# Holding the load of row tile 10 for the transpose of row tile 9 instead of row tile 7

## The chip, the cores and the metric

The kernel runs on one core of a Trainium2 chip. The time is the device time of one execution in microseconds (us), of which the median of several runs is given. The profile is of one execution, with its own time.

## What is computed

```python
batch, m, k, n = 16, 512, 1024, 768
y1 = np.matmul(x, w1)      # x: [16, 512, 1024], w1, w2: [1024, 768], all float32
y2 = np.matmul(x, w2)
out = np.tanh(y1) * y2     # [16, 512, 768], float32
```

Seen as one matrix, x has 8192 rows: 64 row tiles of 128 rows. Both products have the same x, so the weights stand side by side as 1536 columns, three blocks of 512: "a" (the first 512 of w1), "g" (the last 256 of w1 and of w2) and "b" (the first 512 of w2).

## The kernel before, in words

**Tiles.** The first four row tiles (0 to 3) are multiplied plainly, while the weights arrive. The other 60 are taken in 20 triples of three row tiles; the first triple holds rows 4, 5, 6, the second 7, 8, 9, the third 10, 11, 12. For a triple the matrices are seen as 3 row tiles by 2 halves of K, times 2 halves of K by 3 column blocks. That would be 18 block products; the kernel makes 15, out of sums of blocks. A product, called p0 to p14, is four matmuls of 128x512 (`product`, L455). Its left operand is either a half of a transposed row tile or a sum of such halves, called S and a number whose bits name the halves (`A_SUMS`, L13; `x_sum`, L420). S3 is made of the two halves of the triple's first row tile, S11 is S3 less the second half of its second row tile, S15 is made of S11. S11 is read by S15 and p5, S15 by p6 and S31. The right operand is a weight block or a sum B of weight blocks, made once (`w_sum`, L412).

**What a row tile goes through.** From row tile 7 on, each goes through these steps:
- L, the load: GpSimd issues a DMA from memory that also casts to fp16, into one of 8 buffers `xh` (`load_x`, L362).
- D, the sum of absolute values for a check of the inputs' range, on ScalarE (L390).
- T, the transpose: SyncE issues a DMA transpose from `xh` into one of 12 buffers `xT` (L387).
- S, the sums of halves, on VectorE (L421).
- The products on TensorE (L457), with results in PSUM, in 8 banks.
- Copies and sign changes of partial results on ScalarE (`copy`, `seed`, L461), additions of them on VectorE (`add`, L467), tanh on ScalarE (`t`, `th`, L470), the last multiplication on VectorE (`m`, `mh`, L475).
- The store, issued by SyncE (L427).

**Which order.** The order of the products on TensorE is written out by hand (`PE_ORDER`, L69, and `sequence` after it), and neighbouring triples overlap in it. For the other engines a planner (`Planner`, L75 to L224) runs when the kernel is built. It plays the kernel through with assumed costs, and each engine takes the operation that can start first; among those within 0.02 us the one that is due first, and one that is more urgent is waited for (`pick`, L126). It also gives each chain of partial results a PSUM bank. Each engine then executes its list strictly in the planner's order, waiting where an operand isn't there yet: one operation that waits holds up all that stands behind it on its engine.

**What the planner is told of the transposes.** For most transfers it reckons a landing itself. For the transposes of rows 7 to 15 the landing times are written out (`LANDING`, L254; used at L786). They are numbers for the planner's ordering alone: nothing on the chip waits for them.

**The rows' order and the hold.** The rows of the second triple are loaded in the order 7, 9, 8 (`TURNS`, L253; `rows`, L255), those of the third in the order 10, 11, 12. The loads of each triple from the third on are held back: ahead of the triple's first load GpSimd runs a small cast (`hold_loads`, L500, L501) that reads one column of a transposed row tile into a dummy. GpSimd's list is in order, so the loads behind the cast start only when that transpose has landed. Before the change the cast reads the first row tile of the triple before: row 7 for the loads of 10, 11 and 12; row 10 for those of 13, 14 and 15; and so on (L779 to L783):

```python
        if n >= FREE and n % 3 == 0:
            held_by = rows[BY_PE + n - 3]
            op(f"H{mt}", {"pool": 0.1}, None, [f"T{held_by}"], hold_loads, held_by, issued=[before])
            before = f"H{mt}"
```

The load of row 12 also waits until its buffer, that of row 6, is free, and so for the check D of row 6 on ScalarE.

**How operations are named here.** "add4 of the first triple" is operation add4 in the table `C_OPS` for that triple; so with p, S, mh and the others.

Of the kernel before, what the change touches and what calls it, by code (L numbers as in the profile page):

```python
# [74 lines left out]
class Planner:  # L75
# [9 lines left out]
    def op(self, name, engines, due, needs, fn, *args, behind=(), issued=(), chains=(), xfer=0.0, latency=None, seeds=False,  # L85
           lands=None, hold=0.0):
        assert name not in self.ops, name
        self.ops[name] = dict(engines=engines, due=due, needs=[n for n in needs if n], behind=[n for n in behind if n], issued=[n for n in issued if n], fn=fn, args=args,
                              chains=chains, xfer=xfer, latency=latency, seeds=seeds, lands=lands, hold=hold)
        for c in chains:  # L90
            self.chains.setdefault(c, {"left": 0, "bank": None, "end": 0.0, "act": 0.0, "dve": 0.0})["left"] += 1
# [135 lines left out]
def kernel(  # L227
# [18 lines left out]
    BY_PE = HEAD + 3  # L246
# [4 lines left out]
    FILL = 512, 512, 256  # L251
    FREE = 3
    TURNS = (2, 0, 1), (0, 2, 1)  # L253
    LANDING = {7: 35.9, 9: 37.2, 8: 38.4, 10: 45.0, 11: 46.3, 12: 47.7, 13: 54.0, 14: 55.4, 15: 56.8}  # L254
    rows = list(range(HEAD)) + [HEAD + 3 * i + r for i in range(TRIPLES) for r in (TURNS[i] if i < len(TURNS) else (0, 1, 2))]  # L255
    turn = {mt: n for n, mt in enumerate(rows)}
    S_AHEAD, HALVED = 4.0, 4
# [47 lines left out]
    def xh_before(mt):  # L305
        return next((m for m in rows[turn[mt] - 1:1:-1] if xh_place(m) == xh_place(mt)), None)
# [398 lines left out]
    for i in range(TRIPLES):  # L705
# [10 lines left out]
        for o in C_OPS:  # L716
# [22 lines left out]
            if kind in ("t", "th"):  # L739
                lo, n = (0, F) if kind == "t" else (F, G)  # L740
# [11 lines left out]
            else:  # L752
                lo, n, at = (0, F, 0) if kind == "m" else (F, G, G)
# [21 lines left out]
    for n, mt in enumerate(loads):  # L775
        back = xh_before(mt)
        free = [] if back is None else ([f"PT{back}0", f"PT{back}1"] if back < BY_PE else [f"T{back}"]) + ([f"D{back}"] if back >= HEAD else [])
        before = f"L{loads[n - 1]}" if n else last_early
        if n >= FREE and n % 3 == 0:  # L779
            held_by = rows[BY_PE + n - 3]  # L780
            op(f"H{mt}", {"pool": 0.1}, None, [f"T{held_by}"], hold_loads, held_by, issued=[before])
            before = f"H{mt}"
        op(f"L{mt}", {"pool": 0.58}, None, [], load_x, mt, issued=[before], behind=free, xfer=XX)  # L783
    for n, mt in list(enumerate(rows))[BY_PE:]:
        op(f"T{mt}", {"sp": 0.05}, None, [f"L{mt}"], transpose, mt, issued=[f"T{rows[n - 1]}"] if n > BY_PE else [],
           behind=xt_readers[mt - XT_BUFS] if mt >= XT_BUFS and mt - XT_BUFS != HEAD - 1 else [], xfer=1.2, latency=2.0, lands=LANDING.get(mt))  # L786
    for mt in range(HEAD, MT):
# [128 lines left out]
```

## Time and profile before

| | us |
|---|---|
| median of 3 runs | 297.25 |
| the 3 runs | 297.2, 297.25, 298.45 |
| the profiled execution's own time | 297.27 |
| its span, from the first to the last instruction | 295.7 |
| TensorE busy in the span | 289.4 |
| VectorE busy | 255.9 |
| ScalarE busy | 224.3 |
| GpSimd busy | 43.2 |

A line of a timeline gives the start in us from the span's start, the duration in us, the engine (PE is TensorE, PEld its weight load, DVE is VectorE, ACT is ScalarE, POOL is GpSimd, SPq the queue of SyncE), the line of the kernel, the operation, what it writes and reads (`out<-in`, buffer numbers left out), the shapes, and how many like it are merged in the line. In square brackets stand the engine's idle time just before it and what ended that. The durations of neighbours overlap a little, since an engine begins the next operation while the last one drains. A line of a DMA issue ends with the KB of one and the us from issue to landing. A line of the windows gives from:to, the length, then for each engine its busy us and the count of its instructions, the granted clock of TensorE, the DMA share and GB/s.

### The profile page before, as it was taken

Reading aid. Unit: us, or ns where it says so; the run is one execution under the profiler, and the core shown is the slowest. Engines: PE = TensorE matmul, PEld = TensorE weight load, DVE = VectorE, ACT = ScalarE, POOL = GpSimd, SP = SyncE. Lnnn points to the kernel's source line nnn. Section 1 sums busy time; section 2 is a strip of 40 time slices with the busy share of each in tenths; the row PEclk is TensorE's granted clock in tenths of the full one; section 3 lists DMA queues with packets and bytes.
Section 4 is the critical chain, followed back from the end, with each engine's and each line's share of the span. In section 5 each row is a group of like instructions: output and inputs, shape, how many; then the busy total and the mean of one; then the engine's idle time right before and its main releaser. Section 6 shows DMA issues by size and latency. Waiting matters only on the chain. (4 is left out here: it accounts for less than half of the span.)

```text
span 295.7 us, 4593 instructions
## 1 busy us (share of the span) xinstructions
PE 289.4 (98%) x1374; PEld 132.5 (45%) x1374; DVE 255.9 (87%) x552; ACT 224.3 (76%) x454; POOL 43.2 (15%) x94
## 2 busy tenths in 40 slices
PE   7999999999999999999999999999999999999993
PEld 3445444444444444444444444444444444444442
DVE  1679999999989898898989988898888989898884
ACT  2698599799878878877888788677777767778451
POOL 0065112202202022022021120220210100000000
PEclk9999999999999999999999999999999999999999
DMA  6999998999999999999999999999999999041234
GB/s 216 388 323 204 184 153 157 205 240 235 241 177 175 191 242 203 254 174 285 208 200 284 233 230 217 259 270 254 223 296 239 221 280 300 15 162 54 108 142 163
DMA packets 84858, 63.63 MB, mean 215 GB/s; under 512 B 62816, under 2 KB 67168, under 8 KB 84832
## 3 DMA queue, kind: packets, MB, share of 16 engines
q1 hardware_dynamic: 73888, 45.10, 58.8%
q0 software_dynamic: 9936, 16.65, 35.6%
q10 hardware_dynamic: 1008, 1.57, 1.5%
q8 instruction: 11, 0.18, 0.3%
q14 instruction: 15, 0.12, 0.2%
HBM read 39.85 MB, written 25.17 MB: 220 GB/s over the span
## 5 line engine op out<-in xcount | busy, mean ns | idle before, releaser
L457 PE MATMUL bank<-b,early_x 128*128 128x512 f16 x640 | 148.2, 379 | 0.0
L457 PEld LDWEIGHTS <-early_x 128*128 128x128 f16 x800 | 78.2, 98 | 94.5 <-DVE early_x L421 0.3
L467 DVE TENSOR_TENSOR bank<-bank,arena 128x512 f32<-128x512 f32 x100 | 69.7, 697 | 14.7 <-ACT arena L461 12.3
L461 ACT ACTIVATE arena<-bank 128x512 f32<-128x512 f32 x100 | 57.8, 596 | 16.4 <-PE bank L457 16.2
L475 DVE TENSOR_TENSOR o<-o,bank 128x256 f32<-128x256 f32 (+1 forms) x128 | 62.0, 517 | 6.5 <-ACT o L470 4.8
L390 ACT ACTIVATE junk<-xh 128x1024 f16<-128x1024 f16 x60 | 63.4, 1057 | 0.1
L457 PEld LDWEIGHTS <-xT 128*128 128x128 f16 x400 | 39.1, 98 | 46.8 <-issue 0.3
L457 PE MATMUL bank<-b,xT 128*128 128x512 f16 x240 | 58.3, 379 | 0.0
L470 ACT ACTIVATE o<-bank 128x256 f32<-128x256 f32 (+1 forms) x80 | 34.7, 439 | 27.1 <-DVE bank L467 23.7
L457 PE MATMUL bank<-wh,xT 128*128 128x512 f16 x160 | 41.1, 379 | 0.0
L457 PE MATMUL bank<-wh,early_x 128*128 128x512 f16 x160 | 40.9, 379 | 0.0
L362 POOL DMA_DIRECT2D xh<-in_x_dram x61 | 32.4, 542 | 14.9 <-ACT junk L390 7.3
L421 DVE TENSOR_TENSOR early_x<-early_x,xT 128x512 f16<-128x512 f16 x80 | 33.6, 422 | 0.5
L470 ACT ACTIVATE o<-arena 128x512 f32<-128x512 f32 x40 | 25.1, 629 | 8.5 <-DVE arena L467 8.5
L501 POOL CAST held<-xT 128x1 f32<-128x1 f16 x18 | 5.4, 301 | 162.0 <-DMA xT<-xh 162.0
L461 ACT ACTIVATE bank<-bank 128x512 f32<-128x512 f32 x40 | 21.5, 570 | 4.5 <-PE bank L457 3.6
L430 PE MATMUL bank<-wh,xT 128*128 128x512 f16 x72 | 19.6, 379 | 0.2
L421 DVE TENSOR_TENSOR early_x<-xT,xT 128x512 f16<-128x512 f16 x40 | 16.8, 421 | 0.0
L421 DVE TENSOR_TENSOR early_x<-xT,early_x 128x512 f16<-128x512 f16 x40 | 16.8, 420 | 0.0
L467 DVE TENSOR_TENSOR arena<-bank,arena 128x512 f32<-128x512 f32 x20 | 13.7, 687 | 3.0 <-ACT arena L461 3.0
L467 DVE TENSOR_TENSOR bank<-arena,bank 128x512 f32<-128x512 f32 x20 | 13.8, 692 | 0.3 <-PE bank L457 0.3
L467 DVE TENSOR_TENSOR arena<-arena,bank 128x512 f32<-128x512 f32 x20 | 13.6, 681 | 0.0
(51 smaller groups left out, 139.9 us busy)
## 6 DMA issues: line engine op xcount, KB each, us to landing
out_dram<-o SPq DMA_DIRECT2D x59, 384.0 KB, 5.6
xh<-in_x_dram POOLq DMA_DIRECT2D x58, 256.0 KB, 6.7
arena<-in_w_dram SPq DMA_DIRECT2D x12, 256.0 KB, 5.7
early_x<-in_x_dram SPq DMA_DIRECT2D x8, 256.0 KB, 4.8
arena<-in_w_dram ACTq DMA_DIRECT2D x4, 256.0 KB, 5.8
wh<-in_w_dram POOLq DMA_DIRECT2D x8, 128.0 KB, 5.4
xT<-xh SPq DMA_TRANSPOSE x57, 4.6
out_dram<-o SPq DMA_DIRECT2D x3, 256.0 KB, 2.5
```

Source lines behind the costliest of these rows:

```text
L362: pin(nc.gpsimd.dma_start(xh(mt)[:, cols], xf[mt][:, cols]))
L390: pin(nc.scalar.activation(junk[:, :src.shape[-1]], src, ACT.Abs, scale=scale, accum_out=sums[:, column:column + 1]))
L421: pin(engine[e].tensor_tensor(x_operand(i, v), x_operand(i, a), x_operand(i, b), OP[how]))
L430: pin(nc.tensor.matmul(bank(chain)[:, :rhs.shape[-1]], xt(mt)[:, k, :], rhs, start=first, stop=k == KO - 1, skip_group_check=True))
L457: pin(nc.tensor.matmul(place(i, dst), x_operand(i, a)[:, k, :], w_rhs(b, k), start=begins and k == 0, stop=k == KH - 1, skip_group_check=T ...
L461: pin(nc.scalar.activation(place(i, dst), place(i, src), ACT.Copy, scale=float(sign)))
L467: pin(nc.vector.tensor_tensor(place(i, dst), a, b, ALU.add if signs == (1, 1) else ALU.subtract))
L470: pin(nc.scalar.activation(out_tile(HEAD + 3 * i + r)[:, lo:lo + n], place(i, src)[:, :n], ACT.Tanh, scale=float(sign)))
L475: pin(nc.vector.tensor_tensor(o, o, place(i, src)[:, at:at + n], ALU.mult))
L501: pin(nc.gpsimd.tensor_copy(held, xt(mt)[:, 0, :1]))
```

## The change

The cast ahead of the third triple's loads reads row 9 instead of row 7. All later holds are as they were: `n == FREE` is true only for n = 3, which is row tile 10. And the planner is told other landing times for rows 8 and 10 to 15. By these, S11 of the second triple, which needs row 8, can no longer be planned at once behind add128 of the first triple; it stands behind add128 and mh2 of the first triple.

```diff
-    LANDING = {7: 35.9, 9: 37.2, 8: 38.4, 10: 45.0, 11: 46.3, 12: 47.7, 13: 54.0, 14: 55.4, 15: 56.8}
+    LANDING = {7: 35.9, 9: 37.2, 8: 39.4, 10: 47.4, 11: 48.3, 12: 49.2, 13: 55.0, 14: 56.3, 15: 57.6}
...
         if n >= FREE and n % 3 == 0:
-            held_by = rows[BY_PE + n - 3]
+            held_by = rows[BY_PE + n - 3 + (n == FREE)]
             op(f"H{mt}", {"pool": 0.1}, None, [f"T{held_by}"], hold_loads, held_by, issued=[before])
```

## The prediction

> **What bounds the kernel now.** I read the page's engine lines, then the windows of the trace, then who waits for whom, and then the timelines of VectorE, TensorE, GpSimd and the DMA queue around the change.
>
> ```profile
> span 295.7 us, 4593 instructions
> PE 289.4 (98%) x1374; PEld 132.5 (45%) x1374; DVE 255.9 (87%) x552; ACT 224.3 (76%) x454; POOL 43.2 (15%) x94
> ```
> ```profile
> 0.00:14.50 14.50, 12.72 (x69) 6.17 (x70) 5.77 (x15) 6.84 (x12) 0.69 (x6) 1.00 0.84 300
> 14.50:284.00 269.50, 269.50 (x1267) 122.62 (x1266) 243.44 (x525) 214.19 (x436) 42.48 (x88) 1.00 0.99 213
> 291.00:295.70 4.70, 0.16 (x2) 0.00 (x0) 1.06 (x4) 0.00 (x0) 0.00 (x0) 1.00 0.41 142
> ```
>
> The first number of a window row is its length, the second TensorE's busy time. From 14.5 to 284 us TensorE is busy for 269.50 us of 269.50, at a granted clock of 1.00. So TensorE's fixed list of matmuls is the bound, and a wait that the change removes from VectorE, GpSimd or a DMA buys nothing as long as TensorE didn't wait for it. What TensorE has idle is 14.50 - 12.72 = 1.8 us in the lead-in and the 4.7 us tail; the change starts at row tile 10, after 36 us, and touches neither. That is why I look for losses only: **from which point does a later row tile 10 make TensorE wait, and by how much?**
>
> The views of the stretch, first GpSimd's loads and the transposes that they feed:
>
> ```profile
> 35.86 0.37 POOL L501 CAST held<-xT 128x1 f32<-128x1 f16 x1 [7.13 <-DMA xT<-xh]
> 36.37 1.05 POOL L362 DMA_DIRECT2D xh<-in_x_dram  x2
> 38.38 0.53 POOL L362 DMA_DIRECT2D xh<-in_x_dram  x1 [0.96 <-ACT o L470]
> 46.47 0.20 POOL L501 CAST held<-xT 128x1 f32<-128x1 f16 x1 [7.56 <-DMA xT<-xh]
> 47.00 1.59 POOL L362 DMA_DIRECT2D xh<-in_x_dram  x3 [0.33 <-ACT bank L461]
> ```
> ```profile
> 33.78 1.24 SPq L387 DMA_TRANSPOSE xT<-xh  x1
> ```
> ```profile
> xT<-xh SPq DMA_TRANSPOSE x1, 3.3
> ```
> ```profile
> 35.12 1.27 SPq L387 DMA_TRANSPOSE xT<-xh  x1
> ```
> ```profile
> xT<-xh SPq DMA_TRANSPOSE x1, 3.2
> ```
> ```profile
> 40.93 1.23 SPq L387 DMA_TRANSPOSE xT<-xh  x1
> ```
> ```profile
> xT<-xh SPq DMA_TRANSPOSE x1, 5.4
> ```
> ```profile
> 50.71 1.23 SPq L387 DMA_TRANSPOSE xT<-xh  x1
> ```
> ```profile
> xT<-xh SPq DMA_TRANSPOSE x1, 4.2
> ```
>
> Start plus time to landing gives the transposes of rows 9, 8, 10 and 13, in this order: 33.78 + 3.3 = 37.08, 35.12 + 3.2 = 38.32, 40.93 + 5.4 = 46.33 and 50.71 + 4.2 = 54.91 us. The cast at 35.86 is the hold for row 7; the loads of rows 10 and 11 follow at 36.37, that of row 12 at 38.38. The cast at 46.47 is the next hold, for row 10.
>
> **Part 1, the hold.** Nothing is added; one GpSimd cast reads row 9 instead of row 7. Row 9 lands at 37.08. With row 7's spacing (cast 0.1 after the landing, load 0.51 after the cast's start, 36.37 - 35.86) the cast starts at 37.18 and the load of row 10 is issued at 37.69, 1.32 us later. Row 11 stands behind it on GpSimd's queue and moves as much; row 12, issued at 38.38, moves only to 38.74, when the other two (1.05 us) are through. On SP's queue the transposes of 10, 11 and 12 stand behind, then that of 13; the stores come after. When row 10 then lands is not in this trace, so it has two ends. From the same round: the whole 1.32 us goes through, 46.33 + 1.32 = 47.65. From the next round, whose three loads leave back to back as they now will here: 54.91 - 47.00 = 7.91 us after the load, 37.69 + 7.91 = 45.60, earlier than now. I take 47.4, near the upper end, because that row is the same round with the same neighbours, and the lower end only because row 12 moves by 0.36 us, not 1.32.
>
> Who waits for it? VectorE, which runs its list in order:
>
> ```profile
> 47.21 0.43 DVE L421 TENSOR_TENSOR early_x<-xT 128x512 f16<-128x512 f16 x1
> 47.55 0.70 DVE L467 TENSOR_TENSOR bank<-bank,arena 128x512 f32<-128x512 f32 x1
> 48.15 0.89 DVE L421 TENSOR_TENSOR early_x<-early_x,xT 128x512 f16<-128x512 f16 x2
> 48.95 0.75 DVE L475 TENSOR_TENSOR o<-o,bank 128x256 f32<-128x256 f32 x2
> 49.61 0.69 DVE L467 TENSOR_TENSOR bank<-arena,bank 128x512 f32<-128x512 f32 x1
> ```
> ```profile
> 50.78 1.03 PE L457 MATMUL bank<-wh,xT 128*128 128x512 f16 x4
> 53.37 1.03 PE L457 MATMUL bank<-b,early_x 128*128 128x512 f16 x4
> ```
>
> The sum S3 of the third triple (rows 10 to 12) reads row 10 first, at 47.21; S11 and S15 at 48.15 read rows 10 and 11. Their own reader on TensorE is p6 at 53.37, far off. But whatever is queued behind S3 moves with it: add128, S11, S15, two mh, and at 49.61 the addition add4 of the first triple, which ends at 49.61 + 0.69 = 50.30. In the planner's assignment of PSUM banks add4 is the last to read bank 0 before p7 of the third triple takes that bank at 50.78: **0.48 us of slack**, the smallest that I find behind S3. (p7 itself needs row 12 by 50.78; its transpose would land about 1.3 us later than now, by 49.4.) How much of the 0.48 is usable? The nearest that TensorE follows VectorE in this trace:
>
> ```profile
> 30.82 0.42 DVE L421 TENSOR_TENSOR early_x<-early_x,xT 128x512 f16<-128x512 f16 x1
> 31.33 2.75 PE L457 MATMUL bank<-b,early_x 128*128 128x512 f16 x12
> ```
>
> That is 31.33 - 31.24 = 0.09 us. So VectorE may slip by 0.48 - 0.10 = 0.38 us and row 10 may land until 47.21 + 0.38 = 47.59 with no cost. At my 47.4 VectorE slips 0.2 us: cost 0. At the upper end, 47.65: 0.06 us. Beyond that each us of lateness costs TensorE a us, for good, since TensorE has no idle time later to win it back. Below nothing it cannot go.
>
> **Part 2, S11 of the second triple behind add128 and mh2.** It and its neighbours:
>
> ```profile
> 38.24 0.69 DVE L467 TENSOR_TENSOR bank<-bank,arena 128x512 f32<-128x512 f32 x1
> 38.84 0.42 DVE L421 TENSOR_TENSOR early_x<-early_x,xT 128x512 f16<-128x512 f16 x1
> 39.18 0.42 DVE L475 TENSOR_TENSOR o<-o,bank 128x256 f32<-128x256 f32 x1
> 39.51 0.42 DVE L421 TENSOR_TENSOR early_x<-early_x,xT 128x512 f16<-128x512 f16 x1
> 39.84 0.42 DVE L421 TENSOR_TENSOR early_x<-xT,xT 128x512 f16<-128x512 f16 x1
> 40.41 0.70 DVE L467 TENSOR_TENSOR bank<-bank,arena 128x512 f32<-128x512 f32 x1
> ```
> ```profile
> 37.97 0.39 ACT L470 ACTIVATE o<-bank 128x256 f32<-128x256 f32 x1
> ```
> ```profile
> 40.42 1.03 PE L457 MATMUL bank<-b,early_x 128*128 128x512 f16 x4
> ```
>
> These are add128, S11, mh2, S15, S34 and add60. S11 already stands behind add128; it changes places with mh2 alone. mh2 needs the tanh of 37.97, done at 38.36, so it can run at 38.84. S11 then runs from 39.18 to 39.60, and S15, which needs it, no longer has mh2 between: it starts about 39.62 instead of 39.51, ends at 40.04 and is read by p6 at 40.42, with 0.38 us left (over the 0.09 above). S34 ends about 0.1 us later, and the pause before add60 (39.84 to 40.41, where back to back would be 0.33) takes it up. Row 8 landed at 38.32 against 38.84, so S11 did not wait in this execution and there is no stall to remove. Sum: 0. If row 8 landed as late as the new planning number says, 39.4, S11 would start 0.2 us later than 39.18 and S15 would end at 40.26, still ahead of p6; in the old order VectorE would have stood 0.56 us at 38.84, with S15 done at 40.49, and p6 would have paid about 0.2 us.
>
> **Part 3, the later rounds.** The hold on row 10 moves the loads of 13 to 15 by as much as row 10, some 1.1 us, so row 13 lands at about 56.0.
>
> ```profile
> 59.64 0.43 DVE L421 TENSOR_TENSOR early_x<-xT 128x512 f16<-128x512 f16 x1
> ```
>
> Its first reader is at 59.64: 3.6 us are left, so this costs 0. The planner's other times shift by tenths; TensorE's order is written out by hand and stays.
>
> **The sum.** 0 + 0 + 0 on the profiled execution's own 297.27 us (span 295.7 and 1.6 around it), which is the median's 297.25 to within 0.02. I predict 297.3 us. About 0.5%, or 1.5 us, is what a measurement of this kernel can tell from no change.
>
> **The rivals.**
> - *The hold does nothing that VectorE sees.* Row 10 lands as fast as the next round's rows do (45.60 to 47.2), and S3 doesn't move. Time 297.3, the same. For it: the three loads leave closer together. Against it: the row of this round.
> - *A cast that is held up.* The cast has no fixed length: 0.37 us at 35.86, 0.20 at 46.47, and up to 0.65.
>
> ```profile
> 79.36 0.65 POOL L501 CAST held<-xT 128x1 f32<-128x1 f16 x1 [11.03 <-DMA xT<-xh]
> 36.71 1.29 DVE L412 TENSOR_TENSOR b<-b,b 128x1024 f16<-128x1024 f16 x2
> ```
>
> At its new place, 37.18, VectorE is inside two 128x1024 sums (36.71 to 38.0). With 0.65 for 0.37 the load slips 0.28 us more, row 10 lands at 47.65 + 0.28 = 47.93, and TensorE pays 47.93 - 47.59 = 0.34 us: 297.6 us. The Trainium skill's page SBUF — State Buffer, section "SBUF: two separate sides", has a rule for this: a VectorE operation with two SBUF inputs and a GpSimd one that reads SBUF exclude each other for a whole instruction. The short cast at 46.47 and the long ones speak neither clearly for it nor against it; by it the cast would wait for the sum in progress.
> - *Slower.* The same place with a really late row 10: it decides from 47.59, and over 1.5 us are lost from 49.1 on. The longest load-to-landing that the trace shows is that of rows 19 and after, issued at 66.74 and let go by the cast at 79.36: some 12.5 us.
>
> ```profile
> 66.74 1.60 POOL L362 DMA_DIRECT2D xh<-in_x_dram  x3
> ```
>
> With that, row 10 lands at 37.69 + 12.5 = 50.2 and the loss is 50.2 - 47.59 = 2.6 us: 299.9. Against it: that round shared the DMA engines with stores, and no store is issued before 55 us.
> - *Faster.* It would need idle time of TensorE that the change removes; the window rows leave none between 14.5 and 284. Time 297.1 at best, by scatter.
>
> **How the numbers follow.** Forecast (row 10 between 47.2 and 47.7) 0.45; hold unseen, same time, 0.20; a cost of 0.1 to 1.5 us, as in the second rival, 0.22; slower by more than 1.5 us 0.10; faster by over 0.5% 0.03. So within 0.5%: 0.45 + 0.20 + 0.22 = 0.87. The range runs from 297.0 (scatter below the lowest, 297.2) to 298.7 (297.27 and the small-cost rival up to its end), and leaves out 0.13. One of the three times before was 298.45, so 1.2 us can come and go without a change; the range holds that too.
>
> **What would show it.** Right: TensorE busy in the whole of 14.5 to 284 again; the hold's cast near 37.2, the load of row 10 near 37.7, row 10 landing 47.2 to 47.7, VectorE idle 0 to 0.5 us before S3 with "DMA xT<-xh" as what ended it; mh2 ahead of S11 with p6 at 40.42 unmoved. Wrong: an idle time of TensorE or of its weight load near 50.8, with VectorE's add4 as releaser; a row 10 after 49 us; a changed order on VectorE that puts a late row's sum ahead of a chain that TensorE needs; or a wait on row 13 or later.

## The result, and the profile after

The changed kernel takes 297.31 us (median of 22 runs, 296.93 to 298.98). The kernel before, run beside it, takes 298.75 us (median of 22, 297.17 to 300.19), not the 297.25 of the three runs shown ahead of the prediction. The ratio, which is taken over all runs and not from the two medians, is 0.9968, with a 95% interval of 0.9954 to 0.9982: 0.3% faster, within the 0.5% that the prediction took for its margin, but clearly not nothing. That the predicted time, 297.3, is the time that came is luck: the prediction forecast no change, and started from a time *before* that was 1.4 us too short.

The profiled execution of the changed kernel took 297.16 us. First its windows, read as those of before:

```profile
14.50:284.00 269.50, 269.50 (x1269) 122.50 (x1267) 243.50 (x525) 214.28 (x437) 41.62 (x88) 1.00 1.01 213
291.33:295.60 4.27, 0.00 (x0) 0.00 (x0) 0.90 (x3) 0.00 (x0) 0.00 (x0) 0.99 0.47 164
```

TensorE is again busy without a gap from 14.5 to 284 us. The second row begins at the end of the last matmul: the tail lasts 4.27 us. Next GpSimd's casts and loads around the change:

```profile
37.29 0.31 POOL L501 CAST held<-xT 128x1 f32<-128x1 f16 x1 [8.41 <-DMA xT<-xh]
37.80 1.59 POOL L362 DMA_DIRECT2D xh<-in_x_dram  x3 [0.20 <-issue]
46.39 0.38 POOL L501 CAST held<-xT 128x1 f32<-128x1 f16 x1 [7.00 <-DMA xT<-xh]
```

The hold for row 9 lets go at 37.29 and the three loads leave back to back at 37.80, as worked out. But the next hold, which waits for row 10, starts at 46.39, where it started at 46.47 before: row 10 landed no later although its load was issued 1.43 us later (its transpose is issued at 41.40 and takes 4.9 us, so it lands at 46.30; before 46.33). VectorE (first five lines around row 8, then around row 10) and TensorE's p6 and p7:

```profile
38.41 0.69 DVE L467 TENSOR_TENSOR bank<-bank,arena 128x512 f32<-128x512 f32 x1
39.01 0.41 DVE L475 TENSOR_TENSOR o<-o,bank 128x256 f32<-128x256 f32 x1
39.34 0.88 DVE L421 TENSOR_TENSOR early_x<-early_x,xT 128x512 f16<-128x512 f16 x2
40.14 0.42 DVE L421 TENSOR_TENSOR early_x<-xT,xT 128x512 f16<-128x512 f16 x1
40.48 0.70 DVE L467 TENSOR_TENSOR bank<-bank,arena 128x512 f32<-128x512 f32 x1
...
47.31 0.42 DVE L421 TENSOR_TENSOR early_x<-xT 128x512 f16<-128x512 f16 x1
49.24 0.69 DVE L467 TENSOR_TENSOR bank<-arena,bank 128x512 f32<-128x512 f32 x1
```
```profile
40.49 1.03 PE L457 MATMUL bank<-b,early_x 128*128 128x512 f16 x4
50.85 1.03 PE L457 MATMUL bank<-wh,xT 128*128 128x512 f16 x4
```

mh2 (39.01) now stands ahead of S11 (39.34); add60 follows at 40.48 and p6 at 40.49, both 0.07 us later than before. S3 stands at 47.31 against 47.21, p7 at 50.85 against 50.78. Nothing that the change was to touch has gained anything: the last matmul ends at 291.33 us, 0.17 later than before (291.16).

One thing did move that the prediction held fixed. The hand-written order covers the products p; eight of the matmuls that finish row tile 3 (L430, 128x256) are placed between them by the planner, and the new landing times move them. In the kernel before they stand together, in the changed one in three groups:

```profile
287.52 1.04 PE L430 MATMUL bank<-wh,xT_kept 128*128 128x256 f16 x8
```
```profile
283.97 0.27 PE L430 MATMUL bank<-wh,xT_kept 128*128 128x256 f16 x1
284.95 0.60 PE L430 MATMUL bank<-wh,xT_kept 128*128 128x256 f16 x4
288.10 0.49 PE L430 MATMUL bank<-wh,xT_kept 128*128 128x256 f16 x3
```

Whether this other order is what helps is theory E of the experiments.

**Where the time is.** Executions of the kernel before scatter from 297.2 to 300.2, and the profile shown ahead of the prediction (297.27) was one of the shortest. The trace of another execution of the same program, 298.26 us long, shows what a usual one looks like. The same two windows, from 14.5 to 284 and from the end of the last matmul:

```profile
14.50:284.00 269.50, 269.50 (x1268) 122.59 (x1266) 243.49 (x525) 214.27 (x437) 42.23 (x88) 1.00 1.02 213
291.14:296.70 5.56, 0.00 (x1) 0.00 (x0) 0.90 (x3) 0.00 (x0) 0.00 (x0) 0.80 0.36 123
```

and the tail of the short execution of before:

```profile
291.16:295.70 4.54, 0.00 (x0) 0.00 (x0) 0.90 (x3) 0.00 (x0) 0.00 (x0) 1.00 0.42 147
```

TensorE ends at 291.14 in the one and at 291.16 in the other (the granted clock of 0.80 in the tail concerns no matmul, since none runs there). All of the 0.99 us between the two executions (298.26 - 297.27) is in the tail: 5.56 - 4.54 = 1.02 us. The last store tells what is slower in it. Its issue, then its row with the us from issue to landing; first the longer execution of before, then the shorter one, then the changed kernel:

```profile
292.07 0.33 SPq L427 DMA_DIRECT2D out_dram<-o  x1
out_dram<-o SPq DMA_DIRECT2D x1, 128.0 KB, 3.7
```
```profile
292.08 0.60 SPq L427 DMA_DIRECT2D out_dram<-o  x1
out_dram<-o SPq DMA_DIRECT2D x1, 128.0 KB, 2.7
```
```profile
292.26 0.33 SPq L427 DMA_DIRECT2D out_dram<-o  x1
out_dram<-o SPq DMA_DIRECT2D x1, 128.0 KB, 2.3
```

The same 128 KB, issued at 292.07, 292.08 and 292.26, take 3.7, 2.7 and 2.3 us. What else moves at that time stands in the DMA queues. Each row has packets, MB and the share of 16 engines. The longer execution of before, 292 to 294 us:

```profile
q10 hardware_dynamic: 270, 0.37, 52.2%
q1 hardware_dynamic: 272, 0.25, 36.8%
q8 instruction: 1, 0.02, 2.7%
```

the shorter execution of before, 290.9 to 291.1 us:

```profile
q8 instruction: 1, 0.02, 41.9%
```

and the changed kernel, 286 to 288 us:

```profile
q1 hardware_dynamic: 139, 0.31, 40.1%
q8 instruction: 1, 0.02, 3.7%
```

Queues 1 and 10 carry the stores. **Queue 8 carries one packet of 16 KB** now and then, and its time on a DMA engine is long: 41.9% of 16 engines in 0.2 us is 0.419 x 16 x 0.2 = 1.34 us. Its last packet starts at 293.0 us in the longer execution of before, when the last stores are under way; at 290.9 in the shorter one; and at 286.6 in the changed kernel, over 4 us before the last matmul ends. The whole program has 11 such packets. Between the first and the last that come inside TensorE's list, 9 packets apart, TensorE executes 2480 - 204 = 2276 instructions: 253 for a packet. The Trainium skill's page "Trainium Architecture — The Big Picture", section "The software stack", gives an instruction 64 bytes; by that, 16 KB are 256 instructions, and the trace agrees with 253. So I take queue 8 for the fetch of TensorE's instructions. That is an inference from the spacing; no row names the engine.

What is left at the end speaks for such a packet delaying the stores. The DMA queues from 294.0 to 295.4 us, first in the longer execution of before, then in the changed kernel:

```profile
q1 hardware_dynamic: 16, 0.01, 4.2%
q10 hardware_dynamic: 9, 0.01, 1.7%
```
```profile
q1 hardware_dynamic: 17, 0.01, 2.2%
```

One engine of 16 is 6.25%. In the longer execution 4.2 + 1.7 = 5.9%, which is one engine's work, goes on through the whole window, after the other engines are done; in the changed kernel the packets end at 294.2. So the last stores wait for the share of a single engine, as they would if queue 8's packet had held that engine up. The packet there took 27.5% of 16 engines in 0.2 us, 0.88 us; the last store landed 1.4 us later after its issue than in the changed kernel, so the packet's own time doesn't account for all of the delay. Queue 14, whose packets are also of the kind "instruction", is not what differs: it has a packet at 291.7 us in the changed kernel, too.

The changed kernel has one instruction more on TensorE, 2777 against 2776 in the trace: its plan needs 23 waits on semaphores there, the old one 22. If the fetch goes by blocks of some 256 instructions, one instruction at a boundary can decide whether the last block is fetched early or at the very end. The trace fits that: the last packet starts when 2720 of 2777 instructions have started in the changed kernel, and 2773 of 2776 in the longer execution of before.

### The profile page after: what moved, and what is told of

It reads as the page before. It is cut to its first block, busy times and chain, and to the rows that moved or that the text cites. A ratio compares the mean times of both kernels' runs of the same rounds, so it can differ in the third digit from the quotient of the medians.

```text
span 295.6 us, 4588 instructions
## 1 busy us (share of the span) xinstructions
PE 289.5 (98%) x1374; PEld 132.3 (45%) x1374; DVE 255.8 (87%) x552; ACT 224.4 (76%) x454; POOL 42.3 (14%) x94
## 5 line engine op out<-in xcount | busy, mean ns | idle before, releaser
L461 ACT ACTIVATE arena<-bank 128x512 f32<-128x512 f32 x100 | 57.6, 596 | 18.1 <-PE bank L457 18.1
L501 POOL CAST held<-xT 128x1 f32<-128x1 f16 x18 | 4.5, 251 | 161.3 <-DMA xT<-xh 161.3
L461 ACT ACTIVATE bank<-bank 128x512 f32<-128x512 f32 x40 | 21.4, 570 | 4.7 <-PE bank L457 3.9
L430 PE MATMUL bank<-wh,xT 128*128 128x512 f16 x72 | 19.5, 379 | 0.3
L390 ACT ACTIVATE junk<-wh 128x768 f16<-128x768 f16 x16 | 13.6, 847 | 0.1
```

Source lines behind the costliest of these rows:

```text
L390: pin(nc.scalar.activation(junk[:, :src.shape[-1]], src, ACT.Abs, scale=scale, accum_out=sums[:, column:column + 1]))
L430: pin(nc.tensor.matmul(bank(chain)[:, :rhs.shape[-1]], xt(mt)[:, k, :], rhs, start=first, stop=k == KO - 1, skip_group_check=True))
L461: pin(nc.scalar.activation(place(i, dst), place(i, src), ACT.Copy, scale=float(sign)))
L501: pin(nc.gpsimd.tensor_copy(held, xt(mt)[:, 0, :1]))
```

## The experiments

The theories, by the letters that the expectations use. **A**: S11 waited for row 8 in the executions that the first profile did not catch, and the new order saves that. **B**: the same with row 10, bank 0 and p7. **C**: the gain lies elsewhere. After the first four runs, **D**: the fetch of TensorE's instructions collides with the last stores, and an instruction count moves it away. **E**: the new plan gives another order of work in the tail. **F**: the gain lies in the stretch of rows 7 to 15 after all. Ratios are to the kernel before on the same chip, with 95% intervals.

One table for all, each profile's numbers from one execution. The instructions on TensorE are matmuls, as many weight loads, and the waits, with 6 others. "Fetch" is the start of queue 8's last packet, "to the end" its start less the end of the last matmul, "tail" from that end to the span's end.

| kernel | TensorE instructions | fetch | to the end | tail | median us |
|---|---|---|---|---|---|
| before, first profile | 2776 | 290.9 | -0.2 | 4.54 | 298.75 |
| e1_before_again | 2776 | 293.0 | +1.9 | 5.56 | 298.35 |
| e2_hold_only | 2776 | 293.3 | +1.9 | 5.68 | 298.62 |
| e4_s11_only | 2776 | 289.4 | -1.9 | 4.60 | 298.88 |
| e7_after_2less | 2773 | 291.9 | +0.7 | 5.17 | 298.46 |
| e11_after_1less | 2775 | 294.65 | +1.8 | 5.69 | 298.70 |
| after | 2777 | 286.6 | -4.7 | 4.27 | 297.31 |
| e3_plan_only | 2777 | 286.6 | -4.7 | 4.19 | 297.02 |
| e8_before_1more | 2778 | 289.2 | -3.6 | 4.06 | 296.85 |
| e12_after_1more | 2779 | 286.5 | -4.8 | 4.38 | 297.21 |
| e9_before_3more | 2782 | 289.0 | -3.7 | 4.13 | 297.83 |
| e10_after_3more | 2783 | 287.9 | -4.4 | 4.29 | 298.15 |
| e6_before_5more | 2786 | 288.7 | -3.5 | 4.07 | 297.93 |
| e5_before_21more | 2818 | 286.7 | -5.9 | 4.14 | 298.09 |

### e1_before_again

The kernel before, unchanged.

> The kernel before, unchanged, for its scatter (297.17 to 300.19 us in 22 runs, median 298.75) and for a profile that may catch one of its longer executions. Theory A: in the longer ones row 8 is transposed late, VectorE stands at S11 of the second triple (38.84 us in the first profile, no wait there) and TensorE idles 1 to 2 us before p6 of that triple, near 40.4. Theory B: row 10 comes late, VectorE stands at S3 of the third triple (47.21) and TensorE idles near 50.8 (p7 of the third triple, bank 0). Theory C: the loss sits in neither place but in the lead-in or in a later round. Time by all three 297.2 to 300.2, median near 298.7.

Measured: 298.35 us (12 runs), ratio 0.9995 (0.9973 to 1.0016). Its profiled execution, 298.26 us, is the longer one shown above: TensorE is busy for 269.50 of 269.50 us and S11 doesn't cost it anything, so the 1 us is neither at row 8 nor at row 10. It is in the tail.

### e2_hold_only

The hold without the new landing times.

```diff
-            held_by = rows[BY_PE + n - 3]
+            held_by = rows[BY_PE + n - 3 + (n == FREE)]
```

> The hold for row 9 alone, with the old landing times, so that VectorE, ScalarE, TensorE and SyncE have the orders of before. A: the loads of rows 10 and 11 no longer share the DMA engines with the transposes of 9 and 8, row 8 lands by 38.4 always, and the long executions vanish: median 297.3. B: row 10 is about 1 us later than before and the old order meets it at 47.21: median as before or worse, 298.7 to 299.5. C: as before, 298.7.

Measured: 298.62 us, ratio 1.0015 (0.9985 to 1.0045). The hold by itself does nothing for the time. In its profile the cast that reads row 9 took 1.22 us, not 0.31:

```profile
37.15 1.22 POOL L501 CAST held<-xT 128x1 f32<-128x1 f16 x1 [8.48 <-DMA xT<-xh]
```

The load of row 10 left at 38.30 and the next hold let go at 47.14, 0.67 us later than before, and still TensorE was busy for 269.47 of the 269.50 us from 14.5 to 284. So here the prediction's rival of a cast that is held up came about, and cost nothing.

### e3_plan_only

The landing times without the hold.

```diff
-    LANDING = {7: 35.9, 9: 37.2, 8: 38.4, 10: 45.0, 11: 46.3, 12: 47.7, 13: 54.0, 14: 55.4, 15: 56.8}
+    LANDING = {7: 35.9, 9: 37.2, 8: 39.4, 10: 47.4, 11: 48.3, 12: 49.2, 13: 55.0, 14: 56.3, 15: 57.6}
```

> The new landing times alone, with the old hold for row 7: the new order on VectorE, ScalarE and SyncE. A: S11 stands 0.34 us later, so that much of row 8's lateness is forgiven and no more: median between, 297.5 to 298.5. B: the new order and the new banks forgive a late row 10: median 297.3. C, if the loss lies in a later round whose order the new times change: 297.3.

Measured: 297.02 us (296.76 to 298.39), ratio 0.9966 (0.9949 to 0.9982). The whole gain is here. The tail and the last store of its profile (297.11 us):

```profile
291.30:295.50 4.20, 0.01 (x1) 0.00 (x0) 0.91 (x3) 0.00 (x0) 0.00 (x0) 1.00 0.48 167
```
```profile
292.24 0.33 SPq L427 DMA_DIRECT2D out_dram<-o  x1
out_dram<-o SPq DMA_DIRECT2D x1, 128.0 KB, 2.3
```

The matmuls end at 291.30, no earlier than before; the tail is short.

### e4_s11_only

Only row 8's landing time is changed, which moves S11 behind mh2 and leaves the rest of the plan.

```diff
-    LANDING = {7: 35.9, 9: 37.2, 8: 38.4, 10: 45.0, 11: 46.3, 12: 47.7, 13: 54.0, 14: 55.4, 15: 56.8}
+    LANDING = {7: 35.9, 9: 37.2, 8: 39.4, 10: 45.0, 11: 46.3, 12: 47.7, 13: 54.0, 14: 55.4, 15: 56.8}
```

> Of the new landing times that of row 8 alone (39.4 for 38.4), with the old hold: S11 of the second triple behind mh2, rows 10 to 15 planned as before. A: as with all the new times, 297.5 to 298.5. B: as before, 298.7, unless the other bank for p7 helps. C: as before, 298.7.

Measured: 298.88 us, ratio 1.0029 (1.0012 to 1.0047): no gain, if anything a loss. A falls with e2, which should have had the whole gain by it. B falls with the trace of e1, in which TensorE waits nowhere from 14.5 to 284; the times of e2 to e4 alone would fit it. What is left is the rest of the plan. Its tail, its last store, and queue 8 from 289.4 to 289.6 us:

```profile
291.30:295.90 4.60, 0.00 (x0) 0.00 (x0) 0.90 (x3) 0.00 (x0) 0.00 (x0) 0.93 0.50 175
```
```profile
292.22 0.33 SPq L427 DMA_DIRECT2D out_dram<-o  x1
out_dram<-o SPq DMA_DIRECT2D x1, 128.0 KB, 2.7
```
```profile
q8 instruction: 1, 0.02, 34.4%
```

The last store is issued at 292.22, in e3 at 292.24: the order and the times of the tail's issues are the same, TensorE's order from 284 us on too, and yet the medians differ by 1.86 us. That speaks against E. (This profile, 297.55 us, is the shortest of the 12 runs; it doesn't show what a usual run of e4 loses.) What differs is queue 8, at 289.4 here and 286.6 in e3, and TensorE's count, 2776 and 2777.

### e5_before_21more

The kernel before, with none of the change, and 21 more matmuls in the warm-up at the start: 28 of 128 columns in place of 7 of 512, so as many columns. Each matmul brings its weight load, so 42 instructions. The warm-up multiplies constants and nothing reads the results.

```diff
-    WARM = 512, 512, 512, 512, 512, 512, 512
+    WARM = (128,) * 28
...
-        constants(banks[n], cols)
+        constants(banks[n % 8], cols)
```

> The kernel before with its seven warm-up matmuls of 512 columns cut into 28 of 128 columns: the same columns, 21 matmuls and 21 weight loads more, all in the first 5 us; every list behind that is the one of before. What the first four experiments show: TensorE ends at the same time in short and long executions, and the last four stores land 1.0 to 1.4 us later in the long ones, in which the last 16 KB packet of the instruction queue (q8) moves at 293.0 to 293.3 us, among those stores; in the short ones it moves at 286.6 (new planning numbers) or 290.9. Theory D (the fetch of TensorE's instructions, every 256 of them, collides with the last stores): 42 more instructions ahead make the last fetch come about 42 instructions, 4 us, earlier, at 286 to 289; the median falls to 297.0 to 297.5 with nothing else changed. Theory E (the planner's new order of the last operations and stores is what helps): the tail's order is that of before, so as before, 298.4. Theory F (something in rows 7 to 15): as before.

Measured: 298.09 us, ratio 0.9995 (0.9979 to 1.0012), where D expected a gain. Ten of its 12 runs lie within 297.83 to 298.29, a much closer band than that of before. The tail did what D says (4.14 us). But the matmuls end at 292.56 instead of 291.16, since TensorE falls behind by 1.4 us between 21 and 23 us: all of queue 8's packets have moved, and the first now falls at 18.1 us, among the last weight loads. As I read it, the run gives one fetch collision away and buys another; by its time it decides nothing.

### e6_before_5more

The kernel before with `WARM = 512, 512` and ten of 256: five matmuls more.

> The kernel before with five of its seven warm-up matmuls cut in two: 10 instructions of TensorE more. D: the last fetch comes 10 instructions, about 1 us, earlier than in before, at 290 to 292; it now meets the three stores of 288.5 to 289.2 or just clears the last four: between, 297.3 to 298.4. E and F: as before, 298.4.

Measured: 297.93 us, ratio 0.9975 (0.9954 to 0.9996); three runs at 297.0 to 297.1, six at 297.8 to 298.07. The last fetch came at 288.7, earlier than the 290 to 292 expected. Again a short tail, 4.07, and a loss near the start. The last weight load (issue, then time to landing), queue 8 from 20.4 to 20.7 us, and the first stretch of TensorE's list, in e6:

```profile
15.69 0.37 SPq L354 DMA_DIRECT2D arena<-in_w_dram  x1
arena<-in_w_dram SPq DMA_DIRECT2D x1, 256.0 KB, 7.3
```
```profile
q8 instruction: 1, 0.02, 23.9%
```
```profile
14.50:40.00 25.50, 24.90 (x131) 11.54 (x130) 22.65 (x53) 19.27 (x40) 12.36 (x19) 1.00 1.02 216
```

and the same load and stretch in the first profile of before:

```profile
15.58 0.37 SPq L354 DMA_DIRECT2D arena<-in_w_dram  x1
arena<-in_w_dram SPq DMA_DIRECT2D x1, 256.0 KB, 6.0
```
```profile
14.50:40.00 25.50, 25.50 (x136) 11.96 (x135) 23.42 (x55) 20.53 (x41) 10.39 (x20) 1.00 1.09 226
```

In e6 the load takes 7.3 us where it took 6.0, and lands at 22.99 against 21.58. TensorE, which before was busy for all of 25.50 us, comes 5 matmuls less far by 40 us (131 against 136). By these rows the packet of 16 KB does to a load what it does to a store.

### e7_after_2less

The reverse test: the changed kernel with two matmuls fewer, so that the last fetch should move back among the stores. They are short matmuls of constants that fill time; the kernel leaves out no part of the result.

```diff
-    FILL = 512, 512, 256
+    FILL = 512, 512
```

> The changed kernel with 2 of the 6 short matmuls that fill the lead-in left out (those of 256 columns): 4 instructions of TensorE fewer; they write constants that nothing reads. D: the last fetch comes 4 instructions, up to 0.4 us, later than 286.6 if it follows the count alone, and the time stays at 297.1 to 297.3; if it can only come with the end of TensorE's list, it moves to 291 to 293 and the median rises towards 298.4. E and F: 297.3, plus up to 0.2 if TensorE idles in the lead-in.

Measured: 298.46 us (297.35 to 299.14), ratio 0.9998 (0.9974 to 1.0022). The gain is gone with the whole change in place, its hold, its plan and its 23 waits. Tail, last store, and the DMA queues from 291.5 to 293.5 us:

```profile
291.23:296.40 5.17, 0.00 (x0) 0.00 (x0) 0.90 (x3) 0.00 (x0) 0.00 (x0) 0.86 0.40 138
```
```profile
292.15 1.03 SPq L427 DMA_DIRECT2D out_dram<-o  x1
out_dram<-o SPq DMA_DIRECT2D x1, 128.0 KB, 3.2
```
```profile
q10 hardware_dynamic: 255, 0.37, 51.3%
q1 hardware_dynamic: 135, 0.12, 17.6%
q8 instruction: 1, 0.02, 2.7%
q14 instruction: 1, 0.01, 1.5%
```

The matmuls end at 291.23, 0.10 earlier than in the changed kernel; the store takes 3.2 us instead of 2.3, with queue 8's packet among the stores again. F falls with this: rows 7 to 15 are as in the changed kernel.

### e8_before_1more

The kernel before, one warm-up matmul of 512 columns cut in two of 256, which is two instructions more: about the least that D can be tried with, and nothing of the change.

```diff
-    WARM = 512, 512, 512, 512, 512, 512, 512
+    WARM = 512, 512, 512, 512, 512, 512, 256, 256
```

> The kernel before with one of its seven warm-up matmuls cut in two: 2 instructions of TensorE more, the same columns, every list behind that as before. D: the last fetch moves forward by at least those 2 instructions. The changed kernel has just one instruction of TensorE more than the one before (an extra wait) and its last fetch at 286.6, so if the last fetch hangs on the count it jumps here too, ahead of 290.9, and the median falls below 298.0; if it hangs on the order of TensorE's last waits, it stays at 291 to 293 and the median at 298.4. E (order of the tail) and F (rows 7 to 15): as before, 298.4.

Measured: **296.85 us**, ratio 0.9942 (0.9916 to 0.9968), the shortest of all kernels here. It gains at least as much as the change, with the old hold, the old plan and 22 waits: neither the hold nor the new order is needed, and it is the number of instructions, not the wait that came with the plan. Twelve of its 13 runs lie between 296.71 and 297.28. The profiled one is the thirteenth, 298.46: it lost its time in the middle of the kernel (against before, TensorE falls behind by 0.7 us at 163, 0.3 at 167 and 0.2 at 27), not in the tail, which is 4.06 us. No usual run of e8 was profiled. Its last fetch, 289.2 to 289.4 us:

```profile
q8 instruction: 1, 0.02, 27.5%
```

### e9_before_3more and e10_after_3more

The kernel before and the changed one, each with `WARM = 512` four times and six of 256: three matmuls more. If D holds, they should be alike.

> The same with three of the seven cut in two, 6 instructions more. D: the last fetch between that of e8 and that of e6 (288.7); the first fetch stays behind the last load of the g columns (20.6 or later), so there is no loss in the lead-in: 297.0 to 297.9. E and F: 298.4.

> The changed kernel with three of its warm-up matmuls cut in two, 6 instructions more. D: the last fetch at 286 or earlier, still clear of the last stores, fewer executions over 298: 296.9 to 297.3. E and F: 297.3.

Measured: 297.83 us, ratio 0.9978 (0.9955 to 1.0000), and 298.15 us, ratio 0.9978 (0.9955 to 1.0001). They are alike, and both lie between before and e8. For e10 that is a miss: D expected 296.9 to 297.3. For e9 the time is in its range, but not the reason, since no loss near the start was expected. Both have the short tail (4.13, 4.29) and the loss near the start: first fetch at 20.6 and 20.7 us, last weight load landed at 23.05 and 22.93, matmuls ended at 292.67 and 292.31. Over all the traces, a first fetch at 18.1 to 20.7 us goes with a last weight load that lands at 22.9 to 23.05, one at 20.8 to 21.4 with a landing at 21.5 to 21.9.

### e11_after_1less

The changed kernel with one warm-up matmul fewer (it leaves out the seventh, of constants): `WARM = 512` six times.

> The changed kernel with six warm-up matmuls for seven, the seventh left out (it writes a constant that nothing reads): 2 instructions fewer. D: the last fetch between 286.6 (changed kernel) and 291.9 (e7, 4 fewer), the median between 297.3 and 298.5, and higher the later that fetch is. E and F: 297.3.

Measured: 298.70 us, ratio 1.0000 (0.9968 to 1.0032). The last fetch is back among the stores (294.65, tail 5.69), as D says, though later than the 286.6 to 291.9 expected. It isn't a clean test: with the shorter warm-up the matmuls run at half their pace until about 10 us (three fill matmuls take 1.27 us instead of 0.71), and the whole list ends 1.5 us later, at 292.81. e7 is the clean one.

### e12_after_1more

The changed kernel with the warm-up of e8.

> The changed kernel with one warm-up matmul cut in two, 2 instructions of TensorE more, as a version that could beat both. D: TensorE's list is past the count from which the last fetch comes 3.5 us and more ahead of its end (2777 instructions or more in all runs so far; 2776 or fewer put it at the last stores), and the first fetch stays behind the last g load (landing 21.5 to 21.9, not 23): 296.8 to 297.3, no better than e8's 296.85, since the hold and the new order add nothing of their own. If they do add something, 296.6 or less. E and F: 297.3.

Measured: 297.21 us, ratio 0.9972 (0.9952 to 0.9991), as the changed kernel. The fetch was clear of the stores already, so a further instruction buys nothing. The shortest median is that of e8, without hold and new order; the two add nothing to it. Against the changed kernel itself e8 was not compared, and the intervals of their ratios to the kernel before overlap.

**What is shown and what isn't.** Shown: in the execution of 298.26 us the loss of before lies in the last stores' landing, not on TensorE; one matmul more without the change (two instructions) shortens the kernel (e8), and two matmuls fewer with the change (four instructions) take the gain away (e7); the new order on TensorE is not the cause, since e4 has it without the gain and e8 the gain without it; in 14 traces the tail is 4.06 to 4.38 us wherever the last packet of queue 8 starts 3.5 us or more ahead of the end of the matmuls, and 4.54 to 5.69 wherever it starts later. Inferred: that the packet is TensorE's instructions, and that it is the packet that delays the stores (one engine's share of them is late, and the packet holds one engine; that it is the same engine no row says). Open: why, in the same program, the fetch starts at 290.9 us in one execution and at 293.0 in another, what exactly triggers it, and where the single long executions of 300 to 304 us come from.

## Why the prediction was right and wrong

**The hold, right in cost, wrong in the landing.** The cast (37.29 for 37.18) and the loads (37.80 for 37.69) came where they were worked out. Row 10's landing did not: 47.4 was forecast, and it landed at 46.30 (the next hold's cast started at 46.39), within the bounds of 45.60 and 47.65 but nearer the lower. The rival "the hold does nothing that VectorE sees" describes it: S3 moved by 0.10 us, and p7 by 0.07. The choice of the upper end was wrong: three loads that leave together are better matched by the round that also has them together. It cost nothing either way, as e2 confirms.

**S11 and mh2, right.** The swap costs and brings nothing: mh2 at 39.01, S11 at 39.34, p6 at 40.49. e4, the swap without the hold and the later rounds' times, gives no gain.

**The later rounds, right in cost up to 284 us.** TensorE stays busy for 269.50 of 269.50 us. But "TensorE's order is written out by hand and stays" doesn't hold at the end: the matmuls of row 3 stand elsewhere, and the list has 23 waits for 22.

**The step that failed** is the sentence on the 1.8 us of the lead-in and the 4.7 us tail: that the change "touches neither". (The 4.7 us is the length of the window from 291.00; from the end of the last matmul it is 4.54.) From it followed the rival "Faster", which was given 0.03 since only idle time of TensorE could be gained. The tail is not a fixed length. It is the landing of the last stores, and that takes between 2.2 and 3.8 us for the same 128 KB in the 14 traces. The new plan reaches the tail by two ways: it moves work there, which e4 and e8 show to be without effect, and it needs one wait more in TensorE's list. With it the last fetch starts at 286.6 us, where in the kernels of 2776 instructions it starts at 289.4 to 293.3.

**The sum's base failed with it.** The profiled execution, 297.27, and a median of three, 297.25, were taken for the time before; of its 22 runs, 16 lie at 298.4 or above. The row that could have warned stood in the prediction: "one of the three times before was 298.45, so 1.2 us can come and go without a change". It was used as scatter for the range. As far as the profiled executions of before tell (297.27 and 298.26 us), what scatters is the tail with the fetch in it, and a change that removes it gains about that much: 298.75 - 297.31 = 1.44 us. So the forecast time came true by luck: short executions of before were taken for the usual ones, and the changed kernel is as long as those.

## What to carry to other kernels

When the busiest engine has no gap, look at what its end is followed by: a tail of stores has a length of its own, and the DMA queues' rows there, the instruction queue too, tell what it shares the engines with. When three runs of one program differ by more than the effect that is asked for, find out in which window they differ before taking their median for the time. And when a change of order moves the time by a few tenths of a per cent, try an instruction more or less with none of the change (as in e8 and e7) before crediting the order.

## What the runs showed of the hardware

- **A packet of the instruction queue delays data (inferred).** Queue 8's 16 KB packet takes one DMA engine's time for 0.88 us (e1, e7, e8) to 1.34 us (before). With it among them, the last store takes 3.2 to 3.8 us instead of 2.2 to 2.7, and a 256 KB weight load 7.2 to 7.5 instead of 5.9 to 6.1. In e1 what lands last is one engine's share of the stores (5.9% of 16 engines from 294.0 to 295.4 us). The Trainium skill's page "DMA: Bandwidth & Descriptors", section "SWDGE vs HWDGE vs iDMA", calls a packet the boundary at which a DMA engine switches context; a packet of 16 KB that is not left until it is through would hold its engine up like this. The runs agree in direction, but the delays in e1 and e7 (1.4 and 0.9 us against the changed kernel) are longer than or as long as the packet's 0.88 us, and none of them shows the engine's turn itself.
- **The number of instructions moves the time.** 2773 to 2776 on TensorE: 298.35 to 298.88 us. 2777 to 2779: 296.85 to 297.31. 2782 to 2818: 297.83 to 298.15, with the first fetch among the last weight loads.
